# Experts' weights in tiles of 2 MB with 16 KB rows, gate and up of half the features in one tile

## The chip, the cores and the metric

The kernel runs on one core of a Trainium2 chip. The metric is the device time of one launch in microseconds (us). A measurement is the median of several runs; a profiled execution of the same kernel gives the trace. In the views, PE is TensorE (matmul), PEld its weight loads, DVE is VectorE, ACT is ScalarE, POOL is GpSimd and SP is SyncE, the engine that issues nearly all DMAs here.

## The reference, cut to what matters

The network has several blocks in float32, of which the change touches only the last: a mixture of eight experts for 256 tokens of 1024 features, with 3584 hidden features in each expert and the two best experts for a token.

```python
def swiglu(h, w_gate, w_up, w_down):
    return (jax.nn.silu(h @ w_gate) * (h @ w_up)) @ w_down

def moe_swiglu(h, w_router, b_router, w_gate, w_up, w_down):
    logits = (h @ w_router).astype(F32) + b_router.astype(F32)
    top_logits, top_idx = lax.top_k(logits, TOP_K)
    top_w = jax.nn.softmax(top_logits, axis=-1)
    gates = jnp.sum(jax.nn.one_hot(top_idx, N_EXPERTS, dtype=F32) * top_w[..., None], axis=-2)
    out = jnp.zeros(h.shape, F32)
    for e in range(N_EXPERTS):
        y_e = swiglu(h, w_gate[e], w_up[e], w_down[e]).astype(F32)
        out = out + gates[..., e:e + 1] * y_e
    return out.astype(h.dtype)
```

## The kernel before

**Everything ahead of the experts** takes the first 1418 us or so of the span and is the same in both kernels. Weights come there through the helper `w` (L214): one DMA of 1 MB into a tile `raw` of 128 partitions with 8 KB each (L223), and, unless `whole` is set, two casts of 1024 columns to float32r, `hi` (ScalarE, L230), and two differences `lo` = `raw` - `hi` (VectorE, L232). `mm3` (L248) makes one product of float32 accuracy out of three float32r products: hi by hi (L250), lo by hi (L251), hi by lo (L252). The pools of `hi` and `lo` hold six tiles each.

**The experts.** Experts are ranked by the number of their tokens, and rank r has room for `CAPS[r]` = 192, 128, 128, 64, 64, 32, 32, 32 of them. All three matrices of every expert are read, 352 MB in 336 units of 1 MB. An item is one expert and 512 of its hidden features (seven items an expert), 6 MB: two units each of gate, up and down. There are four classes:

- Narrow (ranks 1 and 2, 128 slots): products by `mm3`, so all twelve casts and differences; a silu over 512 columns (L2003), the product with up (L2005), four transposes (L2016) and the split into `hTh` and `hTl` (L281, L282).
- Few (ranks 3 and 4, 64 slots): plain float32 products on the tile as it came (`whole`), in two strips of 64 partitions, at L2049; a silu over 256 columns after gate (L2054), the product with up (L2056) after up, two transposes (L2067), the copy `hTf` (L2073) and the down products (L2080).
- Fewer (ranks 5 to 7, 32 slots): as Few in four strips (L2096), with gate and up in one bank and the silu only after the transpose.
- Wide (rank 0, 192 slots): 128 slots as Narrow and 64 as Few (class Rest), from the same tiles.

The table `order` (L2146 to L2158) sets the order of items: first 14 pairs of Few and Narrow, (3, 1) seven times and (4, 2) seven times, then 21 Fewer with the seven Wide between them. The loop staggers the items: the turned result and the down products of an item come inside the next one.

```python
            if it:
                it.part(0, it.load(0))
                w = it.load(1)
            if last:
                last.prep()
            if it:
                it.part(1, w)
            if last:
                last.down(last.load(2))
                after(last)
            last = it
```

So when a Few item runs, its gate (part 0), the Narrow's transposes (`prep`), the Few's up (part 1) and the Narrow's down follow each other on TensorE; then the next Narrow's gate, the Few's transposes, the Narrow's up and the Few's down.

**Rings and queues.** With the experts the ring of `raw` grows from four tiles of 8 KB a partition by `MORE` = 5, to nine. `unit` (L1975) finds the address of a unit from the expert's number, which SP loads into a register (`value_load`, L1977) when the first unit of that rank is issued. SP issues DMAs in program order, each when its tile of the ring is free. Another register load, of the sum of tokens beyond the room (`over`, L2187), comes after four items; VectorE writes that sum at L2379.

Of the kernel before, what the change touches and what calls it, by code (L numbers as in the profile page):

```python
# [21 lines left out]
MORE = 5  # L22
# [74 lines left out]
def host(inp):  # L97
# [50 lines left out]
    for n in ("gate", "up"):  # L148
        w = g[f"moe_w_{n}_2"][0]
        a["moe_" + n] = np.ascontiguousarray(w.reshape(8, 2, 4, 128, 7, 512).transpose(0, 4, 1, 3, 2, 5)).reshape(112, 128, 2048)  # L150
    w = g["moe_w_down_2"][0]
    a["moe_down"] = np.ascontiguousarray(w.reshape(8, 14, 2, 128, 1024).transpose(0, 1, 3, 2, 4)).reshape(112, 128, 2048)
# [29 lines left out]
class Net:  # L182
    def __init__(self, tc, a, where, es):
        self.tc, self.nc, self.a, self.where = tc, tc.nc, a, where
        p = lambda name, bufs, **k: es.enter_context(tc.tile_pool(name=name, bufs=bufs, **k))
        self.con = p("con", 1)
        self.wp = p("wp", 3)
        self.xp = p("xp", 2)
        self.xt_es = es.enter_context(ExitStack())
        self.sm = p("sm", 3)  # L190
        self.ps = p("ps", 4, space=PSUM)
        self.dr = p("dr", 1, space=DRAM)
        self.xtp = self.xt_es.enter_context(tc.tile_pool(name="xt", bufs=2))
        nc = self.nc
        self.bg, self.more, self.turn = [], None, 0
# [18 lines left out]
    def w(self, src, n=2048, whole=False):  # L214
# [11 lines left out]
        his, los = [], []  # L226
# [611 lines left out]
    def mem_parts(self, l):  # L838

        ms = self.wp.tile([128, 2048], F32, name="raw", bufs=4).rearrange("p (t c) -> p t c", t=2)  # L840
        self.nc.sync.dma_start(ms, self.a["mem"].rearrange("t p c -> p t c"))
        self.norm_t(None, f"norm_mem{l}", 0, out=self.mt, xn=self.rms([ms[:, t] for t in range(2)]))
# [437 lines left out]
    def rwkv_core(self, ph, AR, kt, be, values, vt, ktt, btt, fac, mk, cs, bonus, gv, put):  # L1280
# [18 lines left out]
        with tc.tile_pool(name="rwx", bufs=1) as px:  # L1299
# [27 lines left out]
            def across(c):  # L1327
                MG = MGs[c] = self.wp.tile([128, 2048], F32, name="raw", bufs=4).rearrange("p (h a t) -> p h a t", h=8, a=2)
# [366 lines left out]
    def s5(self, xt, keep, put):  # L1695
# [4 lines left out]
        raw = lambda: self.wp.tile([128, 2048], F32, name="raw", bufs=4)  # L1700
# [131 lines left out]
    def moe(self, xs, rt, out, es):  # L1832
# [150 lines left out]
        class Narrow:  # L1983
# [4 lines left out]

            def load(me, i):
                return [unit(("gate", "up", "down")[i], me.r, 2 * me.f + u) for u in range(2)]  # L1990

            def begin(me):
                me.pn = self.pt()

            def step(me, u, w):
                x = me.xg()
                for k in range(4):
                    self.mm3(me.pn, [q[:, 4 * u + k, me.s * 128:me.s * 128 + 128] for q in x], w(k * 512, 512), u + k == 0, u * 4 + k == 7)

            def finish(me, i):  # L2000
                if i == 0:
                    me.z = ph.tile([128, 512], F32, name="s", bufs=3)
                    nc.scalar.activation(me.z, me.pn, AF.Silu)  # L2003
                else:
                    tt(me.z, me.z, me.pn, op=OP.mult)  # L2005

            def part(me, i, ws):
                me.begin()
                for u, w in enumerate(ws):
                    me.step(u, w)  # L2010
                me.finish(i)
# [8 lines left out]
            def down(me, ws):  # L2020
                f = me.f
                for u, w in enumerate(ws):
                    for j in range(2):
                        for c in range(2):
                            self.mm3(me.acc[c], [q[:, 2 * u + j] for q in me.hT], w(j * 1024 + c * 512, 512), f + u + j == 0, f == 6 and u + j == 2)

        class Few:
# [6 lines left out]
            def load(me, i):  # L2034
                return [unit(("gate", "up", "down")[i], me.r, 2 * me.f + u, True) for u in range(2)]
# [10 lines left out]
            def step(me, u, w):  # L2046
# [4 lines left out]
            def finish(me, i):  # L2051
                if i == 0:
                    me.z = ph.tile([128, 512], F32, name="s", bufs=3)
                    nc.scalar.activation(me.z[:, 0:256], me.pn[:, 0:256], AF.Silu)  # L2054
                else:
                    tt(me.z[:, 0:256], me.z[:, 0:256], me.pn[:, 0:256], op=OP.mult)  # L2056

            def part(me, i, ws):
                me.begin()
                for u, w in enumerate(ws):  # L2060
                    me.step(u, w)
                me.finish(i)
# [12 lines left out]
            def down(me, ws):  # L2075
                c, G = 8 * me.n, 128 // me.n
                for j in range(4):
                    g, b = divmod(j, 2)
                    for o in range(G):
                        mm(me.acc[me.strip(o), 0:c], me.hT[:, b, g], ws[j // 2](j % 2 * 1024 + o * c, c), start=me.f + j == 0, stop=me.f == 6 and j == 3)  # L2080

        class Fewer(Few):
# [3 lines left out]
            def load(me, i):  # L2086
                if i == 2:
                    return Few.load(me, 2)
                return [unit(n, me.r, 2 * me.f + i, True) for n in ("gate", "up")]

            def part(me, i, ws):
                if i == 0:
                    me.begin()
                for k in range(4):
                    for g in range(4):
                        mm(me.pn[me.strip(g), 0:256], me.slots(4 * i + k), ws[g // 2](k * 512 + g % 2 * 256, 256), start=i + k == 0, stop=i + k == 4)  # L2096
# [17 lines left out]
        class Wide(Narrow):  # L2114
# [6 lines left out]
            def part(me, i, ws):  # L2121
                me.begin()
                me.rest.begin()
                for u, w in enumerate(ws):
                    me.rest.step(u, w.raw)
                    me.step(u, w)
                me.rest.finish(i)
                me.finish(i)
# [5 lines left out]
            def down(me, ws):  # L2134
                me.rest.down([w.raw for w in ws])
                Narrow.down(me, ws)
# [15 lines left out]
        for r, f in order:  # L2152
# [327 lines left out]
```

## Time and profile before

| | us |
|---|---|
| median of 3 runs (2285.8 to 2287.61) | 2286.03 |
| profiled execution | 2286.04 |
| its span in the trace | 2284.2 |
| TensorE busy (93% of the span) | 2134.7 |
| VectorE busy (58%) | 1325.0 |
| ScalarE busy (46%) | 1049.5 |

The profiled execution spends 1.8 us outside the span. Its mean granted clock of TensorE is 0.969 of full speed. The busy shares are means over the whole network; the experts are the last 38% of the span, from the first weights at about 1418 us. There the page's 40 slices show some 420 GB/s, against 60 to 291 GB/s in the slices before. For the change, the views that matter are those of the stretches inside this part: the table of stretches, the waits of each engine, and the timeline around one pair.

### The profile page before, as it was taken

To read this page: it belongs to the slowest core of one execution; us is meant where nothing else is said; L and a number is where in the kernel's file an instruction comes from. 1 tells how busy PE (TensorE), PEld (TensorE's weight loads), DVE (VectorE), ACT (ScalarE), POOL (GpSimd) and SP (SyncE) were. 2 spreads that over 40 slices of the span, in tenths; PEclk is the share of its full clock that TensorE was granted. 3 is DMA by queue.
4 is the path that set the end of the run, shared out by engine and by line. 5 is a ranking of instruction groups with operands and counts; after the bars stand their busy time and mean duration, and the time that the engine had idled before them with its cause. 6 is when DMAs were issued, how large, how long until landed. Compare 5 with 4: busy or idle time off the path is not lost.

```text
span 2284.2 us, 36387 instructions
## 1 busy us (share of the span) xinstructions
PE 2134.7 (93%) x14521; PEld 1674.0 (73%) x14521; DVE 1325.0 (58%) x2152; ACT 1049.5 (46%) x1757; POOL 168.6 (7%) x155
## 2 busy tenths in 40 slices
PE   8999999999999789999998898999999999988988
PEld 7779988689987678899988796666666656545544
DVE  5589557677767837555556674555555554333324
ACT  5665455744455446644445553444444443222222
POOL 0000002234400200000001110000000000000000
PEclk9999999999999889999999898999999999999999
DMA  8447644466642346355553241999999999999997
GB/s 291 160 144 253 208 145 180 138 211 221 244 171 95 110 159 227 114 185 185 187 203 111 74 170 60 422 421 421 421 406 420 420 406 394 420 421 421 420 420 314
DMA packets 100317, 593.54 MB, mean 260 GB/s; under 512 B 12003, under 2 KB 25476, under 8 KB 32172
## 3 DMA queue, kind: packets, MB, share of 16 engines
q1 hardware_dynamic: 86528, 562.72, 64.0%
q10 hardware_dynamic: 11596, 17.93, 2.2%
q0 software_dynamic: 2016, 10.49, 1.3%
q8 instruction: 116, 1.90, 0.3%
q14 instruction: 61, 0.50, 0.1%
HBM read 571.40 MB, written 19.69 MB: 259 GB/s over the span
## 4 chain that ended last, share of the span: by engine, by line


## 5 line engine op out<-in xcount | busy, mean ns | idle before, releaser
L232 DVE TENSOR_TENSOR lo<-raw,hi 128x1024 fp32r<-128x1024 f32 x622 | 769.5, 1267 | 335.7 <-ACT hi L230 334.7
L230 ACT CAST hi<-raw 128x1024 fp32r<-128x1024 f32 x622 | 631.6, 1047 | 434.3 <-PE pt L251 166.2
L250 PE MATMUL pt<-xh,hi 128*128 128x256 f32 (+1 forms) x1112 | 315.8, 284 | 3.8 <-DVE xl L284 3.1
L251 PE MATMUL pt<-xl,hi 128*128 128x256 f32 (+1 forms) x1112 | 312.8, 281 | 3.5 <-DVE xl L284 3.5
L252 PE MATMUL pt<-xh,lo 128*128 128x256 f32 (+1 forms) x1112 | 312.7, 281 | 0.0
L250 PEld LDWEIGHTS pt<-xh,hi 128*128 128x128 f32 (+1 forms) x1112 | 210.8, 190 | 9.6 <-issue 3.5
L251 PEld LDWEIGHTS pt<-xl,hi 128*128 128x128 f32 (+1 forms) x1112 | 210.6, 189 | 6.0 <-DVE xl L284 3.9
L252 PEld LDWEIGHTS pt<-xh,lo 128*128 128x128 f32 (+1 forms) x1112 | 210.9, 190 | 0.0
L250 PE MATMUL pt<-hi,xh 128*128 128x256 f32 x512 | 147.5, 288 | 9.7 <-DVE sq L827 4.9
L251 PE MATMUL pt<-lo,xh 128*128 128x256 f32 x512 | 145.1, 283 | 0.0
L252 PE MATMUL pt<-hi,xl 128*128 128x256 f32 x512 | 144.8, 283 | 0.0
L251 PE MATMUL pt<-lo,xgh 128*128 128x512 f32 x336 | 135.8, 404 | 0.9 <-DVE lo L232 0.9
L250 PE MATMUL pt<-hi,xgh 128*128 128x512 f32 x336 | 134.8, 401 | 1.7 <-DVE xgl L284 1.0
L250 PE MATMUL acc<-hi,hhi 128*128 128x512 f32 x344 | 136.0, 395 | 0.0
L251 PE MATMUL acc<-lo,hhi 128*128 128x512 f32 x344 | 135.8, 395 | 0.0
L252 PE MATMUL acc<-hi,hlo 128*128 128x512 f32 x344 | 135.7, 395 | 0.0
L252 PE MATMUL pt<-hi,xgl 128*128 128x512 f32 x336 | 131.2, 390 | 0.0
L2080 PE MATMUL acc<-raw,hTf 128*32 128x256 f32 (+1 forms) x1008 | 123.3, 462 | 7.5 <-DMA raw<-in_moe_down 7.4
L2096 PE MATMUL pt<-raw,xc 128*32 128x256 f32 x1344 | 101.7, 410 | 13.8 <-DMA raw<-in_moe_up 10.4
L250 PEld LDWEIGHTS pt<-hi,xh 128*128 128x128 f32 x512 | 99.5, 194 | 12.8 <-DVE ol L284 6.0
L2049 PE MATMUL pt<-raw,xc 128*64 128x256 f32 x896 | 102.3, 381 | 0.0
L251 PEld LDWEIGHTS pt<-lo,xh 128*128 128x128 f32 x512 | 99.5, 194 | 0.9 <-DVE lo L232 0.3
(686 smaller groups left out, 3624.3 us busy)
## 6 DMA issues: line engine op xcount, KB each, us to landing
raw<-in_moe_gate SPq DMA_DIRECT2D x112, 1024.0 KB, 12.6
raw<-in_moe_up SPq DMA_DIRECT2D x112, 1024.0 KB, 11.5
raw<-in_moe_down SPq DMA_DIRECT2D x112, 1024.0 KB, 12.3
raw<-in_mlp_up SPq DMA_DIRECT2D x32, 1024.0 KB, 5.0
raw<-in_mlp_dn SPq DMA_DIRECT2D x32, 1024.0 KB, 5.0
raw<-in_ff_g SPq DMA_DIRECT2D x11, 1024.0 KB, 4.9
raw<-in_ff_u SPq DMA_DIRECT2D x11, 1024.0 KB, 4.9
raw<-in_ff_d SPq DMA_DIRECT2D x11, 1024.0 KB, 4.9
```

The lines of the kernel that those rows point to most:

```text
L230: nc.scalar.copy(hi[:, :c], raw[:, o:o + c])
L232: nc.vector.tensor_tensor(lo[:, :c], raw[:, o:o + c], hi[:, :c].bitcast(F32), op=OP.subtract)
L250: mm(out, l[0], r[0], start=first, stop=False)
L251: mm(out, l[0], r[1], start=False, stop=False)
L252: mm(out, l[1], r[0], start=False, stop=last)
L2049: mm(me.pn[me.strip(g), 0:256], me.slots(4 * u + k), w(k * 512 + g * 256, 256), start=u + k == 0, stop=u + k == 4)
L2080: mm(me.acc[me.strip(o), 0:c], me.hT[:, b, g], ws[j // 2](j % 2 * 1024 + o * c, c), start=me.f + j == 0, stop=me.f == 6 and j == 3)
L2096: mm(me.pn[me.strip(g), 0:256], me.slots(4 * i + k), ws[g // 2](k * 512 + g % 2 * 256, 256), start=i + k == 0, stop=i + k == 4)
```

## The change

**Weights.** Gate and up of an expert are stored together: `moe_gu` has 112 units of 128 rows by 4096 columns, each with one half of the 1024 input features of gate and, behind it, of up, for 512 hidden features. `moe_down` has 56 such units. A unit is one DMA of 2 MB with rows of 16 KB (L1984 after). The first unit of the first item and the last `down` come as two DMAs of 1 MB into two tiles (`halves`).

**Ring.** The experts have their own ring, `BIG` = 5 tiles of 16 KB a partition. The `raw` tiles of the earlier stages are in a pool of their own, closed before the experts. `in_parts` makes the casts and differences (L231, L233 after) from either kind of tile.

**Items.** Part 0 is the first half of the features for gate and up, part 1 the second half. Narrow keeps two psum tiles; its silu (L2017 after) follows the gate's half of part 1. Few keeps gate and up in one bank, and its `finish` runs after both: one silu over the bank's 512 columns (L2069 after), then the product with up (L2070 after).

```diff
@@ Net.w
-        self.turn = (self.turn + 1) % (4 + MORE) if self.more else 0
-        pool, bufs = (self.wp, 4) if not self.more or 0 < self.turn < 5 else (self.more, MORE)
-        raw = pool.tile([128, 2048], F32, name="raw", bufs=bufs)
+        raw = self.rawp.tile([128, 2048], F32, name="raw", bufs=4)
...
-        his, los = [], []
+        return self.in_parts(raw, n)
...
-        def unit(name, r, i, whole=False):
+        def unit(name, r, i, n, whole, pieces=1):
             if r not in ids:
                 ids[r] = nc.sync.value_load(ints[0:1, 0, r:r + 1], min_val=0, max_val=7)
-            return self.w(a["moe_" + name][bass.ds(ids[r] * 14 + i, 1)].rearrange("o p c -> (o p) c"), whole=whole)
+            src = a["moe_" + name][bass.ds(ids[r] * n + i, 1)].rearrange("o p c -> (o p) c")
+            c = 4096 // pieces
+            raws = [self.more.tile([128, 4096], F32, name="big", bufs=BIG) for _ in range(pieces)]
+            for j, raw in enumerate(raws):
+                nc.sync.dma_start(raw[:, 0:c], src[:, j * c:j * c + c])
+            if not whole:
+                return self.in_parts(raws[0], 4096)
+            return lambda o, n: raws[o // c][:, o % c:o % c + n]
...
+            def part(me, i, w):
                 if i == 0:
+                    me.begin()
+                for j in range(2):
+                    me.half(i, j, w)
+                    if i:
+                        me.finish(j)
...
@@ Few
-            def step(me, u, w):
+            def half(me, i, j, w):
                 for k in range(4):
                     for g in range(2):
-                        mm(me.pn[me.strip(g), 0:256], me.slots(4 * u + k), w(k * 512 + g * 256, 256), start=u + k == 0, stop=u + k == 4)
-
-            def finish(me, i):
-                if i == 0:
+                        mm(me.pn[me.strip(g), j * 256:j * 256 + 256], me.slots(4 * i + k), w(j * 2048 + k * 512 + g * 256, 256), start=i + j + k == 0, stop=i + j + k == 5)
+
+            def finish(me, j):
+
+                if j:
                     me.z = ph.tile([128, 512], F32, name="s", bufs=3)
-                    nc.scalar.activation(me.z[:, 0:256], me.pn[:, 0:256], AF.Silu)
-                else:
-                    tt(me.z[:, 0:256], me.z[:, 0:256], me.pn[:, 0:256], op=OP.mult)
+                    nc.scalar.activation(me.z, me.pn, AF.Silu)
+                    tt(me.z[:, 0:256], me.z[:, 0:256], me.pn[:, 256:512], op=OP.mult)
...
+        items[0].halves, items[-1].halves = ((0, 0),), ((2, 6),)
```

**What moves.** On ScalarE, one pair of items in the first 14 pairs, before: the silu of Narrow (L2003) to the next one.

```order
L2003 ACTIVATE s<-pt 128x512
L230 CAST hi<-raw 128x1024 x2
L281 CAST hTh<-pt 128x512
L2054 ACTIVATE s<-pt 128x256
L230 CAST hi<-raw 128x1024 x6
L2073 COPY hTf<-pt 128x256
L230 CAST hi<-raw 128x1024 x4
```

The same piece of ScalarE's order after the change:

```order
L2017 ACTIVATE s<-pt 128x512
L282 CAST hTh<-pt 128x512
L2069 ACTIVATE s<-pt 128x512
L231 CAST hi<-big 128x1024 x12
L2081 COPY hTf<-pt 128x256
```

The twelve casts of a pair (four for the Narrow's down, eight for the next Narrow's gate and up) stand in one row behind the Few's silu; before, two stood ahead of it, six behind it, and four behind the copy `hTf`.

On SP, at the start of the experts, before: one register load of an expert's number, then the first transfer.

```order
L1977 TENSOR_LOAD ints
L1977 ISA x2
L223 ISA
L223 DMA raw<-in_moe_gate 128x2048
L1277 DMA cap<-in_c_cap 128x8
L223 ISA
L223 DMA raw<-in_moe_gate 128x2048
```

After the change, the last of the eight loads of experts' numbers, the load of `over`, and the first transfers:

```order
L1979 TENSOR_LOAD ints
L1979 ISA x2
L2195 TENSOR_LOAD ints
L2195 ISA x2
L1984 ISA
L1984 DMA big<-in_moe_gu 128x2048
L1984 ISA
L1984 DMA big<-in_moe_gu 128x2048
L1984 ISA
L1984 DMA big<-in_moe_gu 128x4096
```

Seven more loads of experts' numbers stand ahead of these rows, so nine register loads come before the first transfer, where there was one.

## Rows read from the trace of the kernel before

**Rows 1.** Table of stretches, core 0: us; busy us (and count) of each engine; PEclk, DMA share, GB/s

```profile
1445.00:1650.00 205.00, 196.99 (x1087) 131.09 (x1087) 107.26 (x108) 89.54 (x109) 0.00 (x0) 1.00 1.01 421
1905.00:1950.00 45.00, 45.00 (x404) 27.23 (x407) 18.64 (x23) 16.51 (x23) 0.00 (x0) 1.00 1.01 422
1950.00:2260.00 310.00, 278.48 (x2358) 158.60 (x2349) 103.70 (x134) 75.26 (x102) 0.00 (x0) 0.94 1.01 421
```

**Rows 2.** Waits of TensorE, 1445 to 1850 us: total us, times, longest us

```profile
PE acc L251 <- DVE lo L232: 13.7, 13, 1.1
```

**Rows 3.** Waits of TensorE, 1850 to 2285 us

```profile
PE pt L2096 <- DMA raw<-in_moe_up: 10.4, 8, 1.9
```

**Rows 4.** Transposes at L2016, 1480 to 1620 us

```profile
L2016 PE MATMUL pt<-ident,s x20: 272/273/328, 1489.7 to 1609.5; 128*128 128x128 f32 x20
```

**Rows 5.** Timeline of TensorE: start us, us, instruction, idle before and releaser

```profile
1579.84 5.40 PE L2049 MATMUL pt<-raw,xc 128*64 128x256 f32 x48
1585.17 0.73 PE L250 MATMUL acc<-hi,hTh 128*128 128x512 f32 x2
1586.97 0.50 PE L251 MATMUL acc<-lo,hTh 128*128 128x512 f32 x1 [1.07 <-DVE lo L232]
```

**Rows 6.** Timeline of ScalarE

```profile
1581.83 0.39 ACT L2054 ACTIVATE s<-pt 128x256 f32<-128x256 f32 x1 [1.30 <-PE pt L2049]
1582.11 5.78 ACT L230 CAST hi<-raw 128x1024 fp32r<-128x1024 f32 x6
```

**Rows 7.** Timeline of VectorE

```profile
1585.36 0.42 DVE L2056 TENSOR_TENSOR s<-s,pt 128x256 f32<-128x256 f32 x1 [4.10 <-PE pt L2049]
1585.70 6.89 DVE L232 TENSOR_TENSOR lo<-raw,hi 128x1024 fp32r<-128x1024 f32 x6
```

**Rows 8.** Groups by form, ScalarE, 1445 to 1850 us: busy us, mean ns; idle before

```profile
L230 ACT CAST hi<-raw 128x1024 fp32r<-128x1024 f32 x159 | 154.8, 1047 | 0.3 <-PE pt L252 0.3
L2003 ACT ACTIVATE s<-pt 128x512 f32<-128x512 f32 x14 | 8.4, 599 | 18.7 <-PE pt L252 18.7
```

**Rows 9.** Groups by form, VectorE, 1445 to 1850 us

```profile
L232 DVE TENSOR_TENSOR lo<-raw,hi 128x1024 fp32r<-128x1024 f32 x162 | 187.5, 1219 | 29.1 <-ACT hi L230 29.1
```

**Rows 10.** Waits of TensorE's weight loads, 1445 to 1850 us

```profile
PEld pt L251 <- DVE lo L232: 7.7, 22, 0.4
```

**Rows 11.** Table of stretches, columns as in rows 1

```profile
1970.00:1975.00 5.00, 2.46 (x24) 0.89 (x22) 0.00 (x0) 0.00 (x0) 0.00 (x0) 0.89 1.01 419
1975.00:1980.00 5.00, 4.34 (x52) 1.90 (x44) 0.42 (x1) 0.00 (x0) 0.00 (x0) 0.77 1.01 421
1980.00:1985.00 5.00, 3.66 (x25) 2.76 (x26) 2.56 (x3) 3.02 (x4) 0.00 (x0) 1.00 1.02 423
```

**Rows 12.** Timeline of SP's queue: starts of DMA issues

```profile
1417.59 0.37 SPq L223 DMA_DIRECT2D raw<-in_moe_gate  x1
1419.41 0.34 SPq L223 DMA_DIRECT2D raw<-in_moe_gate  x1
1419.95 0.88 SPq L223 DMA_DIRECT2D raw<-in_moe_up  x2
1421.70 0.88 SPq L223 DMA_DIRECT2D raw<-in_moe_gate  x2
```

**Rows 13.** The page, parts 3 and 6: queue of small transfers; lone 1 MB, us to landing

```profile
q10 hardware_dynamic: 11596, 17.93, 2.2%
raw<-in_mlp_up SPq DMA_DIRECT2D x32, 1024.0 KB, 5.0
```

**Rows 14.** Timeline of TensorE at the start of the experts

```profile
1428.88 7.13 PE L2049 MATMUL pt<-raw,xc 128*64 128x256 f32 x64
1441.97 0.50 PE L250 MATMUL pt<-hi,xgh 128*128 128x512 f32 x1 [1.01 <-DVE xgl L284]
```

**Rows 15.** DMA view, 1905 to 2260 us: packets, MB, share of 16 engines

```profile
DMA packets 20475, 149.34 MB, mean 421 GB/s; under 512 B 2268, under 2 KB 2268, under 8 KB 2268
q1 hardware_dynamic: 20446, 148.92, 100.9%
```

More of the change, by code (lines that the diff above doesn't have):

```diff
@@ L21 @@
 D, S, H = 1024, 256, 16
-MORE = 5
+BIG = 5
 CAPS = (192, 128, 128, 64, 64, 32, 32, 32)
@@ L1987, in __init__ @@
                 me.r, me.f, me.xg, me.s, me.acc = r, f, xg, s, acc
+            whole = False
             def load(me, i):
-                return [unit(("gate", "up", "down")[i], me.r, 2 * me.f + u) for u in range(2)]
+                pieces = 2 if (i, me.f) in me.halves else 1
+                return unit("gu", me.r, 2 * me.f + i, 14, me.whole, pieces) if i < 2 else unit("down", me.r, me.f, 7, me.whole, pieces)
+            halves = ()
             def begin(me):
-                me.pn = self.pt()
-            def step(me, u, w):
+                me.ps = self.pt(), self.pt()
+            def half(me, i, j, w):
                 x = me.xg()
                 for k in range(4):
-                    self.mm3(me.pn, [q[:, 4 * u + k, me.s * 128:me.s * 128 + 128] for q in x], w(k * 512, 512), u + k == 0, u * 4 + k == 7)
-            def finish(me, i):
-                if i == 0:
-                    me.z = ph.tile([128, 512], F32, name="s", bufs=3)
-                    nc.scalar.activation(me.z, me.pn, AF.Silu)
-                else:
[L2005 to L2011, printed above, removed]
+                    self.mm3(me.ps[j], [q[:, 4 * i + k, me.s * 128:me.s * 128 + 128] for q in x], w(j * 2048 + k * 512, 512), i + k == 0, i + k == 4)
+            def finish(me, j):
+                if j == 0:
+                    me.z = ph.tile([128, 512], F32, name="s", bufs=3)
+                    nc.scalar.activation(me.z, me.ps[0], AF.Silu)
+                else:
+                    tt(me.z, me.z, me.ps[1], op=OP.mult)
+            def part(me, i, w):
+                if i == 0:
+                    me.begin()
[3 more added lines that the diff above has]
+                        me.finish(j)
             def prep(me):
@@ L2018, in prep, with down @@
                 self.split(p, f3(me.hT[0]), f3(me.hT[1]))
[L2020 to L2027, printed above, removed]
+            def down(me, w):
+                for j in range(4):
+                    for c in range(2):
+                        self.mm3(me.acc[c], [q[:, j] for q in me.hT], w(j * 1024 + c * 512, 512), me.f + j == 0, me.f == 6 and j == 3)
+        class Few(Narrow):
             n = 64
@@ L2032, in __init__ @@
                 me.r, me.f, me.xg, me.acc = r, f, xg, acc
-            def load(me, i):
-                return [unit(("gate", "up", "down")[i], me.r, 2 * me.f + u, True) for u in range(2)]
+            whole = True
             def strip(me, g):
@@ L2073, in prep, with down @@
                 nc.scalar.copy(me.hT.rearrange("p b g c -> p (b g c)"), p[:, 0:256])
-            def down(me, ws):
+            def down(me, w):
                 c, G = 8 * me.n, 128 // me.n
@@ L2079, in down, with part @@
                     for o in range(G):
-                        mm(me.acc[me.strip(o), 0:c], me.hT[:, b, g], ws[j // 2](j % 2 * 1024 + o * c, c), start=me.f + j == 0, stop=me.f == 6 and j == 3)
+                        mm(me.acc[me.strip(o), 0:c], me.hT[:, b, g], w(j * 1024 + o * c, c), start=me.f + j == 0, stop=me.f == 6 and j == 3)
         class Fewer(Few):
             n = 32
[L2086 to L2091, printed above, removed]
+            def part(me, i, w):
                 if i == 0:
@@ L2119, in __init__, with begin, half, finish @@
                 me.rest = Rest(0, f, lambda: got()[2], more)
-            def part(me, i, ws):
-                me.begin()
+            def begin(me):
+                Narrow.begin(me)
                 me.rest.begin()
[L2124 to L2128, printed above, removed]
+            def half(me, i, j, w):
+                me.rest.half(i, j, w.raw)
+                Narrow.half(me, i, j, w)
+            def finish(me, j):
+                me.rest.finish(j)
+                Narrow.finish(me, j)
             def prep(me):
@@ L2132, in prep, with down @@
                 me.rest.prep()
-            def down(me, ws):
-                me.rest.down([w.raw for w in ws])
-                Narrow.down(me, ws)
+            def down(me, w):
+                me.rest.down(w.raw)
+                Narrow.down(me, w)
         acc, wd = ([self.acc() for _ in range(2)] for _ in range(2))
```

30 lines of the change are left out of this document (13 added, 17 removed).

## The prediction

> **What bounds the kernel now.** The change touches only the experts, so I first read the table of stretches over the last 870 us of the span. It falls into two halves. From 1445 to about 1905 us (14 pairs of a Few and a Narrow item) TensorE is busy 196.99 of 205 us, and the DMA engines move 421 GB/s beside it [rows 1]. From 1905 us on (21 Fewer and 7 Wide items) the rate is again 421 to 422 GB/s, but TensorE, after 45 us in which it still works off the ring, is busy only 278.48 of 310 us [rows 1].
>
> Both engines look full in the first half, so the list of waits has to decide. In 1445 to 1850 us TensorE waits 13 times for VectorE's `lo`, 13.7 us, at most 1.1 each, and never for a DMA [rows 2]. After 1850 its largest wait is one for a DMA [rows 3]. **The first half is bound by TensorE, the second by the stream of weights.** What the change does to the order on TensorE, ScalarE and VectorE counts in the first half alone; what it does to the bandwidth counts in the second alone.
>
> The period of a pair gives the scale. The 20 transposes at L2016 are five groups of four; first and last start 119.8 us apart, and three starts inside a group are about 0.4 us, so four pairs take 119.4 and one takes 29.85 us [rows 4]. Twelve units of 1.048576 MB at 421 GB/s take 29.89. DMA just keeps pace, and any wait added on TensorE is a longer pair.
>
> **The place that the change disturbs** is where TensorE goes from a Few item's `up` to the Narrow item's `down`. The Few's 48 products start at 1579.84 and take 5.40, so they end at 1585.24; the two `hi` products run at once; the first `lo` product starts at 1586.97, 1.07 late, for VectorE [rows 5]. ScalarE did its silu of the Few's gate at 1581.83, in the middle of those products, and started the six `hi` casts at 1582.11 [rows 6]. So at 1585.24 the `hi` lay ready. What came late was VectorE: its product with `up` (0.42 us at 1585.36) stands ahead of the `lo`, which start at 1585.70 [rows 7]. The `lo` product started 1586.97 - 1585.24 = 1.73 us after the end of the Few.
>
> **Part 1: one silu after both, in the first half.** The Few item now keeps gate and up in one bank and takes one silu over 512 columns after both. ScalarE works in order, and the excerpt shows all 12 casts of a pair behind this silu, where six of them stood behind a silu that could run 3.4 us before the Few's end. Call that end 0. Silu from 0.12 (the delay from TensorE's end to VectorE's start at 1585.36), 0.60 long [rows 8]. The cast can start about 0.49 after the silu's start, as next instructions on ScalarE start before the former's end (0.28 after a start of 0.39 at 1581.83, so about 0.1 less than its duration) [rows 6]. A cast takes 1.047 [rows 8]: `hi` is there at 0.12 + 0.49 + 1.05 = 1.66, say 1.70. The `lo` takes 1.22 [rows 9]: 2.92, and the product follows at 2.97 against 1.73: **1.24 us more a pair**. The new silu itself is late for nobody else: VectorE's product with `up` fits beside the cast.
>
> Something comes back. Weight loads for the gate products of a Narrow item waited for `lo` 22 times, 7.7 us in all [rows 10], where casts were held up behind the copy `hTf` between them; now 12 casts run in one row ahead of that copy. Of 7.7 us over 13 pairs (0.6 a pair) some was hidden by the running products; I take a third, 0.2. That leaves 1.04 a pair, 13 times: **+13.5 us**. Ends: 0 (had the casts a hidden lead that I don't see) and 13 x 1.24 = 16.1.
>
> **Part 2: the clock.** The granted clock was 1.00 in the first half, with its waits of 1.1 us [rows 1, 2]. In the second half it fell after longer ones: 2.46 us busy of 5 at 0.89, then 4.34 at 0.77, then 1.00 again [rows 11]. In full-clock time that is (0.11 + 0.23) x 5 = 1.7 us lost per fall, from 2.4 to 1.2 GHz for some 3 us. With the new order TensorE stands still for about 1.7 us, runs two `hi` products, and waits 0.8 more; that is between the idle time that kept the clock and that which lost it. No row has just this pattern. Ends: no fall, and a fall in each of 13 pairs, 22.1 us. The total of 2.5 us is that of the slice at 0.89 (2.54 idle), but in two pieces, so I take 8 falls of 13: **+13.6 us**.
>
> **Part 3: the start.** SP loaded one expert's number ahead of the first transfer, at 1417.59; now it loads nine numbers first. Between the issues ending at 1420.83 and starting at 1421.70 lies one such load, 0.87 us, where issues without one are 0.20 apart (1419.75 to 1419.95): 0.67 each [rows 12]. Nine, against one, and the last of them for a sum that VectorE finishes later: about nine times 0.67 later, 1423.6. A lone 1 MB lands 5.0 us after issue [rows 13], each further one 2.49 later (1.048576 MB at 421 GB/s): the Few's fourth MB is there at 1436.1. It is part of a 2 MB tile, so its 32 products (half of 64 in 7.13 us) run after that, to 1439.7. Before, they ended at 1428.88 + 7.13 = 1436.0 [rows 14]: **+3.7 us**, and what follows, up to the first Narrow product at 1441.97, moves with it. Its 2 MB lands at 1441.1 and is cast by 1443.4, before 1445.7, so nothing more. Ends: 0 and the whole delay, 6.0.
>
> **Part 4: 16 KB rows, in the second half.** The units went in 8 KB packets: 355 us of 16 engines at a share of 1.009 for 18178 of them (20446 less 2268 tiny ones) is 315 ns each [rows 15]. The queue of small transfers took 0.022 x 2284.2 x 16 / 11596 = 69.3 ns for 1546 bytes each [rows 13]. The line through both has 12.1 ns fixed and 0.0370 ns a byte: 618.5 for 16 KB against 630.6 for two of 8, 1.9% less. Of 355 us: **-6.8 us**. Ends: 0 (packets may be cut again to 8 KB), and twice as much, -13.6, if nothing fixed is left.
>
> Here a rule weighs in. In the stream 1 MB takes 2.49 us while one alone takes 5.0 [rows 1, 13], so what is fixed per transfer lies beside others. The Trainium skill, "DMA: Bandwidth & Descriptors", section "Anatomy of one DMA — SWDGE (gpsimd) path", prices a transfer at 2.0 us and its bytes at 436 GB/s; taken in a row, every second MB would then save 2 us. The trace disagrees: by that fit 1 MB units could not run at 421 GB/s. By the ceiling of 435 GB/s in the Trainium skill, the same page, "Where 436 GB/s comes from", an estimate, at most 355 x (1 - 421/435) = 11.4 us are to be had; the sum with it would be 2305.4.
>
> The pool for the earlier stages has the four tiles as before, and no instruction ahead of the experts changes its place: nothing. The last `down` still comes in 1 MB pieces: nothing.
>
> **Sum.** 13.5 + 13.6 + 3.7 - 6.8 = +24.0 on the profiled execution's 2286.04 (span 2284.2 and 1.8 around it), which is the median of the runs, 2286.03: **2310.0 us**.
>
> **Rivals.**
> *B, the stall without the clock.* The two `hi` products inside the wait keep the clock at 1.00. For it: waits of 1.1 us did no harm [rows 2]. Against: the wait doubles. 2310.0 - 13.6 = 2296.4.
> *C, not slower.* The casts don't end up on TensorE's path, because the pair has slack elsewhere that takes it up; it decides at a new wait of under (6.8 - 3.7) / 13 = 0.24 us a pair. For it: VectorE and ScalarE are busy half the time in this half [rows 1]. Against: TensorE's 197 of 205 us leave no slack. 2286.0 + 3.7 - 6.8 = 2282.9; with nothing fixed left in a packet, -13.6, it is 2276.1, faster. By the ceiling of the Trainium skill, "DMA: Bandwidth & Descriptors", "Where 436 GB/s comes from", an estimate, it would be 2278.3.
> *D, 16 KB rows give nothing,* since the engines are at a limit of bytes and not of packets: 2310.0 + 6.8 = 2316.8. For it: the share is 1.009 already.
> *E, the ring is too coarse.* Five tiles come free in steps of 2 MB, and a Wide item holds one through four casts and four subtractions (4 x 1.22 = 4.9 us). If the stream ran dry for 2 us in each of seven Wide items, 14 us: 2324. Against: ten MB of ring are more than the nine of before.
>
> **How the numbers follow.** A 0.45, B 0.22, C 0.16 (half of it under 2281.4), D 0.11, E 0.06. A measurement tells some 0.2%, 4.6 us, from no change. Faster by more: half of C and a little for what I overlook, 0.10. Within: the rest of C and B with a smaller stall, 0.13. Slower: 0.77. The range of 2284 to 2320 holds A, B and D with their ends, and leaves out most of C and E.
>
> **What would show it.** Right: the waits of the first `lo` product for `lo` grow from 1.07 to about 1.3 behind a new wait of about 1.7 for the `hi` cast, 13 times; a pair takes 30.9 us or more; the clock falls under 1.00 in some slices between 1445 and 1905; the stream of the second half runs at about 429 GB/s; the first transfer is issued near 1423.6. Wrong: pairs of 29.9 us still, TensorE waiting for DMA in the first half, or 421 GB/s and gaps in the stream of the second half.

## The result and the profile after

The changed kernel takes 2299.76 us (median of 11 runs, 2288.61 to 2305.59) against 2286.92 (11 runs, 2284.12 to 2290.31): a ratio of 1.0052 with a 95% interval of 1.0040 to 1.0064, so about 12 us slower. The forecast was slower, 2310.0 in a range of 2284 to 2320. The profiled execution took 2298.85, with a span of 2297.2; the differences below are between the spans, 13.0 us.

The page of the changed kernel, its span and the busy times:

```profile
span 2297.2 us, 35656 instructions
PE 2125.8 (93%) x14521; PEld 1681.7 (73%) x14521; DVE 1320.9 (57%) x2152; ACT 1054.8 (46%) x1757; POOL 168.6 (7%) x155
```

The busy time of TensorE is nearly that of before, and so are those of the other engines. The table of stretches of the changed kernel answers to [rows 1]; columns as there:

```profile
1445.00:1650.00 205.00, 191.38 (x1041) 130.33 (x1042) 104.44 (x105) 87.95 (x104) 0.00 (x0) 0.99 1.00 423
1650.00:1700.00 50.00, 44.77 (x244) 30.14 (x241) 27.52 (x30) 23.71 (x29) 0.00 (x0) 0.97 0.90 350
1905.00:1950.00 45.00, 44.28 (x377) 27.26 (x376) 17.83 (x21) 14.46 (x19) 0.00 (x0) 1.00 0.92 380
1950.00:2260.00 310.00, 270.77 (x2415) 161.14 (x2416) 99.16 (x133) 74.69 (x100) 0.00 (x0) 0.94 1.00 424
```

In 1445 to 1650 us TensorE's busy time fell by 5.6 us while the stream still moved 423 GB/s. The granted clock is 0.99 and 0.97 in the first two stretches. From 1650 to 1700 the stream drops to 350 GB/s, and from 1905 to 1950 to 380: SP waits there for tiles of the ring that VectorE's differences and TensorE's products still hold. The kernel before had such pauses too, 404 GB/s from 1650 to 1700 and 376 from 1850 to 1905.

The waits of TensorE, 1460 to 1870 us (total us, times, longest), which answer to [rows 2]:

```profile
PE acc L251 <- ACT hi L231: 21.2, 13, 1.6
PE acc L252 <- DVE lo L233: 6.8, 13, 0.5
```

The 13 waits of 1.07 us for `lo` have become 13 of 1.63 for `hi` and 13 of 0.52 for `lo`: 28.0 us against 13.7. The largest wait of TensorE after 1870 us is again for a DMA [rows 3]:

```profile
PE pt L2099 <- DMA big<-in_moe_gu: 14.7, 7, 2.6
```

The transposes of a Narrow item (as in [rows 4], for the same count of five groups):

```profile
L2033 PE MATMUL pt<-ident,s x20: 272/273/328, 1495.7 to 1618.5; 128*128 128x128 f32 x20
```

Four pairs take 1618.5 - 0.4 - 1495.7 = 122.4 us, one takes 30.6, against 29.85. The timeline around one such place, TensorE first (start us, us, instruction, idle before and releaser), answers to [rows 5]:

```profile
1557.31 3.67 PE L2063 MATMUL pt<-big,xc 128*64 128x256 f32 x32
1562.62 0.73 PE L251 MATMUL acc<-hi,hTh 128*128 128x512 f32 x2 [1.63 <-ACT hi L231]
1563.88 0.50 PE L252 MATMUL acc<-lo,hTh 128*128 128x512 f32 x1 [0.53 <-DVE lo L233]
```

The Few's last 32 products start at 1557.31 and take 3.67, so they end at 1560.98. The first `lo` product follows at 1563.88. ScalarE and VectorE at that place, which answer to [rows 6] and [rows 7]:

```profile
1561.04 0.60 ACT L2069 ACTIVATE s<-pt 128x512 f32<-128x512 f32 x1 [3.03 <-PE pt L2063]
1561.53 11.48 ACT L231 CAST hi<-big 128x1024 fp32r<-128x1024 f32 x12
```

```profile
1561.67 0.42 DVE L2070 TENSOR_TENSOR s<-s,pt 128x256 f32<-128x256 f32 x1 [2.94 <-ACT s L2069]
1562.60 13.71 DVE L233 TENSOR_TENSOR lo<-big,hi 128x1024 fp32r<-128x1024 f32 x12 [0.51 <-ACT hi L231]
```

The silu starts 0.06 us after the Few's end, the casts 0.49 after the silu, the first difference at 1562.60, when the first cast is done. This is the chain that the prediction had laid out: 2.90 us from the Few's end to the first `lo` product, where it had 2.97. The wait for `lo` in it is 0.53, where the prediction had 0.8 in one place and 1.3 in another; its own chain leaves 0.54, from 1.70 and two `hi` products of 0.73 together to 2.97. No weight load for a gate or up product waits for `lo` any more in this stretch [rows 10].

The clock falls in the first half, where it had not fallen before. Two slices of 5 us around one of the falls:

```profile
1465.00:1470.00 5.00, 3.37 (x28) 1.88 (x24) 1.55 (x3) 2.17 (x3) 0.00 (x0) 1.00 1.01 429
1470.00:1475.00 5.00, 4.47 (x13) 3.45 (x13) 5.00 (x5) 5.00 (x7) 0.00 (x0) 0.66 0.99 423
```

There were three such falls, at 1444, 1471 and 1659 us. The price shows between the transposes of successive pairs: 32.2 us (1463.5 to 1495.7) with the fall at 1471, where the next takes 30.5, so about 1.6.

SP's first transfer of experts' weights, which answers to [rows 12]:

```profile
1422.51 2.90 SPq L1984 DMA_DIRECT2D big<-in_moe_gu  x5
```

The DMA view of 1920 to 2180 us, which answers to [rows 15]:

```profile
DMA packets 7608, 110.86 MB, mean 426 GB/s; under 512 B 840, under 2 KB 840, under 8 KB 840
q1 hardware_dynamic: 7588, 110.56, 100.1%
```

With 840 tiny packets left out, 6748 packets of 16 KB are left: 260 us x 16 x 1.001 / 6748 = 617 ns each. The stream runs at 426 GB/s instead of 421.

### The profile page after: what moved, and what is told of

Read it like the earlier page. It is cut to its first block, busy times and chain, and to the rows that moved or that the text cites. A ratio compares the mean times of both kernels' runs of the same rounds, so it can differ in the third digit from the quotient of the medians.

```text
span 2297.2 us, 35656 instructions
## 1 busy us (share of the span) xinstructions
PE 2125.8 (93%) x14521; PEld 1681.7 (73%) x14521; DVE 1320.9 (57%) x2152; ACT 1054.8 (46%) x1757; POOL 168.6 (7%) x155
## 4 chain that ended last, share of the span: by engine, by line
## 5 line engine op out<-in xcount | busy, mean ns | idle before, releaser
L233 DVE TENSOR_TENSOR lo<-raw,hi 128x1024 fp32r<-128x1024 f32 x370 | 476.6, 1300 | 253.0 <-ACT hi L231 252.7
L231 ACT CAST hi<-raw 128x1024 fp32r<-128x1024 f32 x370 | 383.7, 1046 | 364.9 <-PE pt L252 166.9
L233 DVE TENSOR_TENSOR lo<-big,hi 128x1024 fp32r<-128x1024 f32 x252 | 289.5, 1219 | 52.9 <-ACT hi L231 52.7
L231 ACT CAST hi<-big 128x1024 fp32r<-128x1024 f32 x252 | 243.5, 1048 | 68.8 <-DMA big<-in_moe_gu 67.3
L2088 PE MATMUL acc<-big,hTf 128*32 128x256 f32 (+1 forms) x1008 | 122.8, 480 | 13.8 <-DMA big<-in_moe_down 13.2
L2088 PEld LDWEIGHTS acc<-big,hTf 128*32 128x32 f32 (+1 forms) x1008 | 45.5, 125 | 77.9 <-issue 64.2
```

The costliest lines, as they stand in the source:

```text
L231: nc.scalar.copy(hi[:, :c], raw[:, o:o + c])
L233: nc.vector.tensor_tensor(lo[:, :c], raw[:, o:o + c], hi[:, :c].bitcast(F32), op=OP.subtract)
L2088: mm(me.acc[me.strip(o), 0:c], me.hT[:, b, g], w(j * 1024 + o * c, c), start=me.f + j == 0, stop=me.f == 6 and j == 3)
```

## Experiments

Each run was timed in five rounds against the kernel before on the same chip. Runs 3, 4, 6 and 8 were on another chip than 1, 2, 5 and 7; the differences of medians between runs that are given below agree with those of the ratios, except where it is said.

**1. The late silu alone, in the kernel before.** Units of 1 MB, 8 KB rows and the ring of nine stay; only class Few changes (and, through it, the Few part of a Wide item).

```diff
-            def begin(me):
-                me.pn = self.pt()
+            def begin(me, i=0):
+                me.i = i
+                if i == 0:
+                    me.pn = self.pt()
...
-                        mm(me.pn[me.strip(g), 0:256], ...
+                        mm(me.pn[me.strip(g), me.i * 256:me.i * 256 + 256], ...
...
             def finish(me, i):
-                if i == 0:
+                if i:
                     me.z = ph.tile([128, 512], F32, name="s", bufs=3)
-                    nc.scalar.activation(me.z[:, 0:256], me.pn[:, 0:256], AF.Silu)
-                else:
-                    tt(me.z[:, 0:256], me.z[:, 0:256], me.pn[:, 0:256], op=OP.mult)
+                    nc.scalar.activation(me.z, me.pn, AF.Silu)
+                    tt(me.z[:, 0:256], me.z[:, 0:256], me.pn[:, 256:512], op=OP.mult)
```

> The kernel before, with units of 1 MB, 8 KB rows and its ring of nine, in which only the Few item is changed: gate and up in one bank and one silu over 512 columns after both. Theory (late silu): a wait for hi of about 1.6 us and one for lo of 0.5 take the place of the 1.07 for lo, a pair takes 29.85 + 1.24 = 31.1 us, since the small waits of the weight loads (0.59 a pair) stay; 13 x 1.24 = +16 and up to 8 clock falls of 1.7: 2299 to 2316. Rival (ring): pairs of 29.9 us, 2285 to 2289.

Measured: 2307.27 us (6 runs), ratio 1.0087 (1.0068 to 1.0106). The waits of TensorE, 1460 to 1870 us, and the transposes of this run:

```profile
PE acc L250 <- ACT hi L230: 21.2, 13, 1.6
PE acc L251 <- DVE lo L232: 6.9, 13, 0.5
```

```profile
L2016 PE MATMUL pt<-ident,s x20: 272/273/329, 1491.3 to 1617.5; 128*128 128x128 f32 x20
```

The waits are those of the changed kernel to about a tenth. Undisturbed intervals between pairs are 31.05 us, 1.20 more than before, where 1.24 had been worked out; of the five groups shown one interval holds a fall of the clock and takes 32.65. The late silu by itself costs more than the whole change. What the change takes back is 0.5 us a pair. The weight loads' waits for `lo` are still here, as in [rows 10]; in the changed kernel, whose casts stand in one row, they are gone. Weight loads of this run, 1460 to 1870 us:

```profile
PEld pt L251 <- DVE lo L232: 7.7, 22, 0.4
```

**2. The casts first, in the changed kernel.** The down tile's casts and differences are queued ahead of the Few's silu and product.

```diff
-                    nc.scalar.activation(me.z, me.pn, AF.Silu)
-                    tt(me.z[:, 0:256], me.z[:, 0:256], me.pn[:, 256:512], op=OP.mult)
+                    with ExitStack() as st:
+                        for ins in self.ahead:
+                            st.enter_context(tc.issue_after(ins))
+                        nc.scalar.activation(me.z, me.pn, AF.Silu)
+                        tt(me.z[:, 0:256], me.z[:, 0:256], me.pn[:, 256:512], op=OP.mult)
...
+            self.ahead = ()
             if last:
                 last.prep()
+                w2 = last.load(2)
+                if it and it.r in (3, 4):
+                    self.ahead = (self.cast, self.sub)
             if it:
                 it.part(1, w)
             if last:
-                last.down(last.load(2))
+                last.down(w2)
```

Here `issue_after` queues what it encloses behind an instruction of the same engine; `cast` and `sub` are the last ones that `in_parts` made.

> The changed kernel, but the Narrow's down tile is taken up, and its four casts and four differences queued, ahead of the Few's silu and product on ScalarE and VectorE; the order on TensorE and SP stays. Theory (late silu): the waits of the first down products for hi (21.2 us, 13 times) and lo (6.8, 13 times) go, a pair falls from 30.55 us to what the stream then allows, 12.58 MB at 427 GB/s = 29.5, and the clock no longer falls between 1440 and 1880 us: 13 x 1.05 + 5 = 19 us less than the changed kernel at most, 2281 to 2287. Rival (the ring of 2 MB tiles is what holds the first half back): waits for DMA take the place of those for hi, pairs stay at 30.5 us, 2297 to 2300.

Measured: 2278.5 us (12 runs, 2275.31 to 2285.69), ratio 0.9968 (0.9957 to 0.9979): faster than both kernels, by 8 us than before. The waits of TensorE, the transposes and two stretches:

```profile
PE acc L252 <- DVE lo L233: 5.2, 9, 1.0
PE acc L251 <- ACT hi L231: 4.0, 7, 1.7
```

```profile
L2033 PE MATMUL pt<-ident,s x20: 272/273/328, 1489.2 to 1606.8; 128*128 128x128 f32 x20
```

```profile
1445.00:1650.00 205.00, 200.01 (x1111) 135.85 (x1109) 110.16 (x112) 93.73 (x112) 0.00 (x0) 1.00 1.01 427
1905.00:1950.00 45.00, 44.45 (x401) 27.15 (x403) 17.78 (x22) 14.43 (x19) 0.00 (x0) 1.00 1.01 428
```

The waits fall from 28.0 to 9.2 us, four pairs take 117.2 us (29.3 each), and the stream runs at 427 GB/s through both stretches without a pause. The order behind the Few's silu was the cause of the loss: run 1 puts it in alone and loses, this run takes it out and gains. The run moves VectorE's differences along with ScalarE's casts, so the two engines are not told apart, and the wait for `lo` of the kernel before goes with them (run 8).

The time lies below the theory's 2281 to 2287 us. A pair takes 28.0 us at first (transposes at 1461.14 and 1489.16), while the ring is ahead, and 29.0 to 29.8 in the next four; 12.58 MB at 427 GB/s take 29.5. The casts now wait for the stream, in 1460 to 1870 us:

```profile
ACT hi L231 <- DMA big<-in_moe_down: 21.4, 11, 3.6
```

The theory had no fall of the clock between 1440 and 1880 us; there were two, between 1440 and 1445 and between 1820 and 1825 us.

**3. The casts first, with 8 KB rows.** Each 2 MB tile is filled by two DMAs.

```diff
-                nc.sync.dma_start(raw[:, 0:c], src[:, j * c:j * c + c])
+                for h in range(0, c, 2048):
+                    nc.sync.dma_start(raw[:, h:h + 2048], src[:, j * c + h:j * c + h + 2048])
```

> The run with the casts first (2278.5 us), with every 2 MB tile filled by two DMAs of 1 MB with rows of 8 KB; the tiles, the ring and all orders stay. Theory (longer rows carry the stream from 421 to 427 GB/s): the stream goes back to 421, pairs that follow the stream take 29.9 us, and 352 MB take 838 instead of 826 us: about 12 us more, 2288 to 2291. Rival (fewer issues or the larger ring carry it): the stream stays at 427, 2277 to 2280.

Measured: 2287.39 us (12 runs), ratio 1.0007 (0.9993 to 1.0021), 8.9 us above run 2, from which its interval is apart (the theory had 2288 to 2291; the profiled executions lie 5.7 us apart in their spans):

```profile
1445.00:1650.00 205.00, 199.67 (x1107) 135.19 (x1105) 112.70 (x112) 96.58 (x114) 0.00 (x0) 1.00 1.01 421
1905.00:1950.00 45.00, 45.00 (x368) 27.67 (x367) 18.04 (x22) 14.58 (x18) 0.00 (x0) 1.00 1.01 421
```

The stream is back at 421 GB/s with the same tiles, ring and orders. The length of the rows, or the size of a transfer that goes with it, gives the 427; the two were not told apart. The number of bytes that the ring holds does not give it.

**4. The casts first, with a ring of four.** `BIG = 4`.

> The run with the casts first, with a ring of four tiles of 16 KB instead of five. Theory (the ring is deep enough at five, since 2 MB take 10.6 us from issue to landing and 4.9 us in the stream, so two to three are under way): at four some 2 to 3 are under way and one to two are being used, and the stream begins to pause: 5 to 20 us more, 2283 to 2298. Rival (five is already too coarse): a loss of 2 MB would stop the stream in every pair, over 1 us for each of 28 items and more in the second half, over 30 us more.

Measured: 2300.01 us (6 runs), ratio 1.0062 (1.0042 to 1.0082), 21.5 us above run 2. Two stretches, and the largest wait of TensorE after 1870 us:

```profile
1445.00:1650.00 205.00, 200.03 (x1102) 137.21 (x1103) 111.14 (x112) 95.41 (x113) 0.00 (x0) 0.98 1.01 427
1950.00:2260.00 310.00, 259.47 (x2246) 152.31 (x2246) 94.28 (x125) 69.43 (x92) 0.00 (x0) 0.92 0.97 402
```

```profile
PE acc L2091 <- DMA big<-in_moe_down: 24.3, 11, 3.1
```

The pairs hardly feel it: from the first transposes of a Narrow to the last they take 385.7 us, where run 2 takes 385.6, though they begin 3.8 us later. The second half does: 402 GB/s, and TensorE waits 24.3 us for `down` tiles. So four tiles are too few for it. The loss lies just above the 5 to 20 us of the theory; the over 30 us that the rival asked for were not reached, and its place was wrong too.

**5. Products in the gap, first try.** Seven products that nothing reads, between up and down.

```diff
+            if it and last and it.r in (3, 4) and last.r in (1, 2):
+                p = self.pt()
+                x = last.xg()[0]
+                for k in range(7):
+                    mm(p, last.hT[0][:, 0], x[:, 0:2].rearrange("p a b -> p (a b)"), start=k == 0, stop=k == 6)
```

> The changed kernel, with seven more products of 128x512 float32r into a psum tile that nothing reads, between a Few item's up and the Narrow's down (13 or 14 times); seven at 0.2275 us fill the wait of 1.63 us for the hi cast. The sum computed is the same. Theory (the clock falls because TensorE stands still there): the wait for hi shrinks to near 0, pairs stay at 30.5 to 30.7 us, the clock stays 1.00 between 1445 and 1880 us, and the time falls by the three falls, about 5 us, to 2293 to 2297, with less spread among runs. Rival (falls have another cause, or the spread of the runs comes from elsewhere): as many falls, 2299 to 2302, spread of 15 us as before.

Measured: 2333.3 us (5 runs), ratio 1.0196 (1.0174 to 1.0219). Both theories missed it:

```profile
1565.44 1.89 PE L2207 MATMUL pt<-xgh,hTh 128*128 128x512 f32 x7 [0.68 <-ACT hTh L282]
1567.27 3.67 PE L2063 MATMUL pt<-big,xc 128*64 128x256 f32 x32
1572.57 0.73 PE L251 MATMUL acc<-hi,hTh 128*128 128x512 f32 x2 [1.63 <-ACT hi L231]
```

The seven products were issued ahead of the Few's second part, where they wait 0.68 us for the Narrow's hidden values, and the old wait of 1.63 stays. From the Narrow's transposes to these last products of the Few it is now 3.16 us (1564.11 to 1567.27), where the changed kernel takes 0.58 (1556.73 to 1557.31): 2.6 us a pair, and the time is 33.5 us above the changed kernel for 13 pairs, 2.6 each. As a test of the clock it failed; as a test of the bound it says that time added on TensorE in the first half comes out whole.

**6. Products in the gap, held in place.** As run 5, with the block inside `tc.issue_after(self.up)`, where `up` is the last product of the Few's up.

> The changed kernel with the seven products that nothing reads held, on TensorE, directly behind the last product of the Few's up (the earlier try had them issued ahead of it, where they waited for the Narrow's hidden values). The sum computed is the same. Theory (the clock falls because TensorE stands still there): the wait for hi shrinks to near 0, pairs stay at 30.5 to 30.7 us, no clock falls between 1450 and 1880 us, and the time falls by the two or three falls of 1.6 us each, to 2294 to 2297. Rival (the falls have another cause): as many falls, 2299 to 2302.

Measured: 2297.05 us (7 runs, 2284.79 to 2300.28), ratio 1.0033 (1.0013 to 1.0053). TensorE at one place, the transposes, and two stretches:

```profile
1561.99 1.88 PE L2208 MATMUL pt<-xgh,hTh 128*128 128x512 f32 x7
1563.71 0.71 PE L251 MATMUL acc<-hi,hTh 128*128 128x512 f32 x2
1564.96 0.50 PE L252 MATMUL acc<-lo,hTh 128*128 128x512 f32 x1 [0.53 <-DVE lo L233]
```

```profile
L2033 PE MATMUL pt<-ident,s x20: 272/273/328, 1496.7 to 1619.5; 128*128 128x128 f32 x20
```

```profile
1450.00:1650.00 200.00, 196.14 (x1068) 134.47 (x1068) 101.39 (x102) 85.75 (x103) 0.00 (x0) 1.00 1.01 427
1650.00:1700.00 50.00, 48.04 (x269) 32.70 (x266) 28.95 (x32) 24.33 (x30) 0.00 (x0) 1.00 0.91 358
```

The filling takes the place of the wait to the hundredth: the first `hi` product starts 5.32 us after the Few's last products do (1558.39 to 1563.71), where it was 5.31 with the wait, and a pair still takes 122.4 / 4 = 30.6 us. The clock is 1.00 from 1450 to 1850 us, where the changed kernel has 0.99 and 0.97. One profile without a fall would prove little, as run 7 has only one in the same pairs. But in all ten profiles (both kernels and eight runs) every fall between 1460 and 1905 us stands at such a gap, behind a wait of about 1.6 us for `hi` and one of 0.5 for `lo`; the kernel before, whose waits there are at most 1.1, and this run have none. So the falls come from TensorE standing still, at some of the gaps. Their worth, 2.7 us between the medians (4.3 by the ratios) against 3.2 for two falls, lies within the intervals of the two ratios, so only the traces show it.

**7. Experts' numbers loaded late.** In the changed kernel; `sent` is the last transfer that SP has issued.

```diff
-                ids[r] = nc.sync.value_load(ints[0:1, 0, r:r + 1], min_val=0, max_val=7)
+                with tc.issue_after(self.sent) if ids else ExitStack():
+                    ids[r] = nc.sync.value_load(ints[0:1, 0, r:r + 1], min_val=0, max_val=7)
...
+                with tc.issue_after(self.sent):
+                    over = nc.values_load(ints[0:1, 2, 0:1], min_val=0, max_val=512)
```

> The changed kernel, with each expert's number loaded on SP only behind the transfer ahead of its first use, and the sum of tokens beyond the room behind the transfers of the first four items, as before. Theory (late start costs): the first transfer goes out at about 1417.6 instead of 1422.5 us, the first transposes of a Narrow come 3 to 4 us earlier, 2295 to 2297. Rival (the start is hidden behind the gather of the tokens, which ends at 1428.5 anyway): the first products start as now, 2299 to 2301.

Measured: 2301.45 us (6 runs), ratio 1.0066 (1.0047 to 1.0084), no better than the change. SP's first transfer, and SP's wait ahead of it in 1416 to 1424 us:

```profile
1421.59 3.25 SPq L1985 DMA_DIRECT2D big<-in_moe_gu  x5
```

```profile
SPq L1985 <- DVE pk L2354: 3.5, 1, 3.5
```

The loads are out of the way, and the transfer still goes out at 1421.59: it waits 3.5 us for an instruction of VectorE that writes `pk`, a tile of the router (L2354, at 1421.15). VectorE writes `pk` again at 1424.2, after the transfer, so that tile is not the reason. The same instruction is the last to read `pos`, a tile in a pool that is closed ahead of the experts; that the new pool lies where it was is likely, but it was not moved to see. So the transfer was not early in this run, and what an early one would be worth stays untested.

**8. The kernel before, with its own wait taken away.** VectorE's first two differences for the Narrow's down stand ahead of the Few's product with up.

```diff
                 else:
-                    tt(me.z[:, 0:256], me.z[:, 0:256], me.pn[:, 0:256], op=OP.mult)
+                    with ExitStack() as st:
+                        for ins in self.ahead:
+                            st.enter_context(tc.issue_after(ins))
+                        tt(me.z[:, 0:256], me.z[:, 0:256], me.pn[:, 0:256], op=OP.mult)
...
             if last:
                 last.prep()
+                w2 = last.load(2)
+                if it and it.r in (3, 4):
+                    self.ahead = (self.subs[-3],)
```

Of the four differences of the tile, `subs[-3]` is the second.

> The kernel before, with only one thing changed: on VectorE the first two differences for the Narrow's down stand ahead of the Few's product with up, so that the 13 waits of 1.07 us for them go. Theory (two limits lie at the same height): TensorE alone would need 28.8 us a pair, but twelve units of 1 MB at 421 GB/s need 29.9, so waits for DMA take their place, pairs stay at 29.8 to 29.9 us, and the time at 2284 to 2288. Rival (TensorE alone bounds the first half, as the prediction had it): pairs of 28.8 us, 13 us less, 2271 to 2276.

Measured: 2281.84 us (12 runs), ratio 0.9977 (0.9963 to 0.9991). The transposes of three pairs at the beginning of the first half, and two stretches:

```profile
L2017 PE MATMUL pt<-ident,s x12: 272/273/328, 1488.9 to 1546.3; 128*128 128x128 f32 x12
```

```profile
1445.00:1650.00 205.00, 202.19 (x1111) 135.90 (x1111) 113.06 (x114) 93.53 (x113) 0.00 (x0) 1.00 1.01 421
1950.00:2260.00 310.00, 276.23 (x2315) 156.42 (x2314) 100.72 (x133) 73.78 (x100) 0.00 (x0) 0.92 1.01 418
```

Neither theory holds as it stood. The pairs do fall, to (1546.3 - 0.4 - 1488.9) / 2 = 28.5 us, but only as long as the ring is ahead; later ones take 29.6 to 29.9, at 421 GB/s all along. The last Narrow's transposes come 9.1 us earlier than before (1846.7 against 1855.8), and the span ends only 2.9 earlier (2281.3 against 2284.2): the stream, which never stopped, takes the rest back in the second half.

The interval of this run overlaps that of run 2 (0.9957 to 0.9979). So once this wait is gone from both kernels, a gain of the 2 MB tiles over the old ones is not shown.

## Why the prediction was right, and where its terms were off

The sign and the main mechanism, the stall, were right. The 13.0 us between the spans can be placed by the first `lo` product of each Narrow's down. (The transposes don't serve for this: before, 16 of the Few's products stood ahead of them, now 32 do, 1.8 us more.) The first and the last of the 14, before:

```profile
1467.53 0.50 PE L251 MATMUL acc<-lo,hTh 128*128 128x512 f32 x1 [0.99 <-DVE lo L232]
1862.05 0.50 PE L251 MATMUL acc<-lo,hTh 128*128 128x512 f32 x1 [1.04 <-DVE lo L232]
```

And after the change:

```profile
1470.67 0.50 PE L252 MATMUL acc<-lo,hTh 128*128 128x512 f32 x1 [0.53 <-DVE lo L233]
1876.19 0.50 PE L252 MATMUL acc<-lo,hTh 128*128 128x512 f32 x1 [1.02 <-DVE lo L233]
```

The changed kernel is 3.1 us late at the first, 14.1 at the last and 13.0 at the end, so 1.1 comes back in the second half. Of the 14.1, the three falls of the clock are 4.8 and the late start 0.3 (Part 3); 9.0 are left for the stall.

- **Part 1, the stall.** Its chain was right in each link, and 1.24 us a pair is what run 1 shows alone (1.20). What comes back was undersized: a third of the 7.7 us in [rows 10] was taken, and run 1 against the changed kernel says 0.5 a pair, nearly all. So 0.7 a pair, 9.0 us, in place of 13.5.
- **Part 2, the clock.** The price of a fall was right (1.6 us for 1.7), and so was its cause (run 6). The number was off: two in the pairs of the profiled execution, and three with the start, in place of eight. The 2.5 us of idle time lie in two pieces with two products between them, and most times that kept the clock. This is the largest error of the sum: 13.6 forecast, 3.2 measured in the pairs.
- **Part 3, the start.** 3.7 us forecast, 0.3 measured. The delay of the first transfer was near (1422.5 for 1423.6), and so was the end of the Few's products (1440.2 for 1439.7). That what follows moves with it was wrong: TensorE ran products of the tokens' gather (L1867) while it waited for the Few's second tile, products that stood behind the Few's before. The first product of the Narrow came at 1442.25, where it had come at 1441.97 [rows 14]:

```profile
1436.58 3.67 PE L2063 MATMUL pt<-big,xc 128*64 128x256 f32 x32
1442.25 0.49 PE L251 MATMUL pt<-hi,xgh 128*128 128x512 f32 x1 [1.12 <-ACT hi L231]
```

The fall at 1444 us, 1.6, which the prediction did not have, came on top. The reason given for the late transfer, nine register loads, is not the only one, since without them it is only 0.9 us earlier (run 7).

- **Part 4, the rows.** The packet of 16 KB was priced at 618.5 ns and took 617. But the engines' share fell from 1.009 to 1.001, so the stream gained 1.2% (426 for 421) instead of 1.9: 4.2 us of 355. Measured were 1.1. Each kernel's stream pauses once near the start of the second half, the changed one at 380 GB/s from 1905 to 1950 us, the one before a little earlier:

```profile
1850.00:1905.00 55.00, 52.76 (x412) 31.58 (x412) 28.26 (x44) 19.29 (x33) 0.00 (x0) 1.00 0.95 376
```

So the pause does not explain the difference; where the rest of the 4.2 went was not followed up. In run 3 the same step shows in a kernel whose stream does not pause, and is worth 8.9 us there.

- **"The first half is bound by TensorE, the second by the stream."** Half of this was wrong. For time that is added in the first half it holds (runs 1 and 5: all of it comes out). For time that is taken away it does not: in run 8, 9.1 us won there became 2.9 at the end. The period of a pair, 29.85, and its transfers, 29.89, lay so near each other that both limits counted; the prediction saw this and drew the one-sided conclusion.
- **The rivals.** B, the stall without falls, 2296.4, was near the result, as most gaps kept the clock. C fell with the first timeline. D falls with run 3, which does not tell the length of the rows from the size of a transfer. E, a ring too coarse, was not what happened here (424 GB/s from 1950 to 2260 us), but run 4 shows it one tile away.
- **The total.** It came nearer than its terms, which is luck. Parts 1 to 3 were too high by 4.5, 10.4 and 3.4 us; against that stand 5.7 that the second half did not give back and 1.6 of a fall that was not in the sum.

The rule of the Trainium skill ("DMA: Bandwidth & Descriptors", "Anatomy of one DMA — SWDGE (gpsimd) path"), a fixed 2.0 us for each transfer, was fitted there to single DMAs that GpSimd issued. It does not show in this stream, which SP issues: transfers of 1 MB in run 3 and of 2 MB in run 2 differ by 421 to 427 GB/s, as the prediction expected of several in flight.

## What to carry to other kernels

When gate and up are joined, look at what stood behind the earlier of the two results on each in-order engine: here a silu of 0.6 us took twelve casts with it, and the loss was larger than the gain for which the tiles were joined. Queue the conversions of the next step ahead of an activation that has time; that turned a loss of 12 us into a gain of 8. Then give the old version the same order before the gain is put down to the tiles: run 8 did, and came too near to run 2 to tell them apart. And where two limits lie within a per cent of each other, a wait that is added counts whole, a wait that is removed counts only until the other limit is reached.

## What was not expected

- The eleven runs of the changed kernel spread over 17 us (2288.61 to 2305.59), those of the kernel before beside them over 6. The two fastest had a granted clock of 0.972, the others 0.963 to 0.968, which would fit gaps that lower the clock in some executions and not in others. But run 6, whose first gap is filled, spreads over 15.5 us (2284.79 to 2300.28, clock 0.965 to 0.973) and run 8 over 14.7, and 24 runs of the kernel before in a later round spread over 11. So the gaps are not shown to cause the spread; its cause stays open.
- The DMA engines' share of 16 engines' time is 1.009 with 8 KB packets and 1.001 with 16 KB; so a packet twice as long cost 617 ns against 2 x 315, 2% less, while the stream gained 1.2%.
- In run 7 the first transfer into a new pool waited 3.5 us for an instruction of an earlier stage, which nothing in the new code names; that the pool lies where a tile of that stage was is likely and was not tried.
